# One PSUM bank instead of two pools for the latent head transposes of a two-layer hybrid decoder

## The chip, the core and the metric

The kernel runs on one core of one Trainium2 chip. The metric is the device time of one execution in microseconds (us). Five engines work beside each other, each through its own queue in program order: TensorE (PE, the matrix engine; its weight loads are listed as PEld), VectorE (DVE), ScalarE (ACT), GpSimd (POOL) and SyncE (SP), which issues most DMAs. PE writes its results to PSUM, which the kernel divides into eight tiles of 128 partitions by 512 floats, one bank each.

## What is computed

Two layers, each with a norm, one wide projection, three token mixers (a gated short convolution, multi-head latent attention, dilated window attention), gates, and an output projection with a residual. 512 tokens, width 1024. The part around the change is the latent attention, eight heads with 96 columns for queries and keys and 64 for values:

```
q = (rmsnorm(c_q, q_a_norm_g) @ w_uq).reshape(B, S, MLA_HEADS, MLA_QK)
kv = (rmsnorm(c_kv, kv_a_norm_g) @ w_ukv).reshape(B, S, MLA_HEADS, MLA_NOPE + MLA_V)
k_nope, v = jnp.split(kv, [MLA_NOPE], axis=-1)
k = jnp.concatenate([k_nope, jnp.broadcast_to(k_pe[:, :, None, :], ...)], axis=-1)
q = rmsnorm(q, mla_q_norm_g)
k = rmsnorm(k, mla_k_norm_g)
...rotary embedding on the last 32 columns of q and k...
o_b = causal_block_attention(q, k, v, MLA_QK ** -0.5)
```

## The kernel before

Matrix products are made from three matmuls (lines 124 to 126) on operands that are split into a rounded high part (`hi`, a cast on ACT) and a remainder (`lo`, a subtraction on DVE).

**Heads in pairs.** For each of the four head pairs `p`, `mla_p1` projects queries, keys and values and normalizes them with tokens on the partitions, and `mla_p2` turns queries and keys so that the 96 columns lie on the partitions. `mla_p2` makes four steps: the queries of head 0 (called q0 below), its keys (k0), the queries of head 1 (q1), its keys (k1). A step is four PE transposes into one PSUM tile (line 490), then a scaled cast on ACT that reads the tile (`hi`, line 494), then a scaled subtraction on DVE that reads it too (`lo`, line 495). The tile can be written again when line 495 is done. After each step `mla_p2` yields.

**What lies between the steps.** PE's order is written out by hand and is the same whatever the tiles are. A generator `filler` holds the wide projections (three matmuls of 512 columns for each advance). In the first `mla_p2` of a layer (`p` = 0, before the attention loop) two advances stand between steps. The other three run inside `mla_main`, which mixes scores (`mla_scores`), transposes of the probabilities (`mla_trans`, line 526), products with the values (`mla_pv`) and one step of `mla_p1` or `mla_p2` at a time, with one or two advances of `filler` between any two. The order on ACT, DVE and POOL is set by a scheduler at build time, by priorities.

**PSUM.** One pool with five tags gives the eight banks: `pj` two (projections), `sc` two (scores), `tr` two, `pv` one, `p1` one. `tr` holds the transposed probabilities, the query steps of `mla_p2`, the dilated queries (`dil_t`, line 680, its first half) and some small work. `p1` holds the products of `mla_p1`, the key steps of `mla_p2` and the dilated keys. In the trace and in the order below `p1` is written `p`, since numbers at a name's end are left out.

In the stretch that matters, a query step and the next key step use different banks, so PE can transpose the keys while ACT and DVE still read the queries. The probabilities and the query steps share the two `tr` banks in turn.

```
def psum(tag):
    return pp.tile([P, 512], F32, tag=tag, name=nm(tag), bufs=1 if tag in ("pv", "p1") else 2)
```

Of the kernel before, what the change touches and what calls it, by code (L numbers as in the profile page):

```python
# [49 lines left out]
def hybrid_kernel(ctx: ExitStack, tc: tile.TileContext, a: dict):  # L50
# [13 lines left out]
    def nm(s):  # L64
        uid[0] += 1
        return f"{s}_{uid[0]}"

    def psum(tag):
        return pp.tile([P, 512], F32, tag=tag, name=nm(tag), bufs=1 if tag in ("pv", "p1") else 2)
# [4 lines left out]
    def t2(shape, dt=F32):  # L74
        return sp.tile(shape, dt, tag="c2", name=nm("c2"), bufs=C2)
# [90 lines left out]
    def tok_nat(c):  # L166
        return slice(c * P, (c + 1) * P)
# [47 lines left out]
    ps = psum("tr")  # L215
# [6 lines left out]
    for l in range(DEPTH):  # L222
# [257 lines left out]
        def mla_p2(p):  # L480
            m = mla[p]
            for h in range(2):
                qk = []
                m["qk"].append(qk)
                for i in range(2):
                    ps = psum("p1" if i else "tr")
                    for c in range(NCH):
                        o = (2 * (p % 2) + h) * 96
                        src = m["kv"][c // 2][:, c % 2, h * P:h * P + 96] if i else m["q"][:, c, o:o + 96]
                        nc.tensor.transpose(ps[:96, tok_nat(c)], src, ident)  # L490
                    g = prm[:96, O_MK:O_MK + 1] if i else prm2[:96, 27:28]
                    hi, lo = t2([P, S], F32R), t2([P, S], F32R)
                    qk += [hi, lo]
                    nc.scalar.activation(hi[:96], ps[:96], AF.Copy, scale=g)
                    nc.vector.scalar_tensor_tensor(out=lo[:96], in0=ps[:96], scalar=g, in1=hi[:96],
                                                   op0=ALU.mult, op1=ALU.subtract)
                    yield
# [59 lines left out]
        def mla_main():  # L557

            prep = iter(())

            def more():
                if next(prep, "end") is None:
                    yield False

            for n in range(32 + LAG + PV_LAG + 1):
                for p in range(1, 4):
                    if n == P1_AT[p - 1]:
                        drain(prep)
                        mla_prep_w(p)
                        prep = mla_p1(p)  # L570
                    if n == P2_AT[p - 1]:
                        drain(prep)
                        prep = mla_p2(p)
                if n < 32:
                    mla_scores(n)
                    yield n >= N_TAIL
                yield from more()
                if 0 <= n - LAG < 32:
                    mla_trans(n - LAG)
                    yield n >= N_TAIL  # L580
                yield from more()
                i = n - LAG - PV_LAG
                if 0 <= i < 32 and i % 2 == 1:
                    mla_pv(i // 2)
                    yield n >= N_TAIL
# [435 lines left out]
        for _ in mla_p2(0):  # L1021
            advance(fill, 2)
# [19 lines left out]
        for dt in range(KD):  # L1042
# [4 lines left out]
            ps = psum("pj")  # L1047
# [103 lines left out]
```

## Time and profile before

| | |
|---|---|
| median of 3 runs | 1430.21 us (1429.95 to 1430.77) |
| the profiled execution | 1431.0 us, its span 1429.2 us |
| PE busy | 1419.2 us, 99% of the span |
| DVE, ACT, POOL busy | 874.0, 696.9, 121.4 us (61%, 49%, 8%) |
| DMA | 136.53 MB, 34.0% of the engines' time on the main queue |
| TensorE clock | granted share 0.998 over the run |
| chain of work that ended last | PE 92%, DVE 3% |

In a timeline row stand the start in us from the span's start, the duration in us, the engine, the line, the operation, and the tiles (out<-in) with shapes and count. A last bracket, where there is one, gives the time for which the engine sat idle just before and what it waited for. Rows of equal instructions that follow each other are merged into one; PE rows overlap since matmuls are pipelined.

### The profile page before, as it was taken

Reading aid. Unit: us, or ns where it says so; the run is one execution under the profiler, and the core shown is the slowest. Engines: PE = TensorE matmul, PEld = TensorE weight load, DVE = VectorE, ACT = ScalarE, POOL = GpSimd, SP = SyncE. Lnnn points to the kernel's source line nnn. Section 1 sums busy time; section 2 is a strip of 40 time slices with the busy share of each in tenths; the row PEclk is TensorE's granted clock in tenths of the full one; section 3 lists DMA queues with packets and bytes.
Section 4 is the critical chain, followed back from the end, with each engine's and each line's share of the span. In section 5 each row is a group of like instructions: output and inputs, shape, how many; then the busy total and the mean of one; then the engine's idle time right before and its main releaser. Section 6 shows DMA issues by size and latency. Waiting matters only on the chain.

```text
span 1429.2 us, 20412 instructions
## 1 busy us (share of the span) xinstructions
PE 1419.2 (99%) x7258; PEld 1174.1 (82%) x7258; DVE 874.0 (61%) x2298; ACT 696.9 (49%) x1587; POOL 121.4 (8%) x149
## 2 busy tenths in 40 slices
PE   9999999999999999999999999999999999999998
PEld 8888888888787878788898888888878878787887
DVE  7786877466363766455576858865654647564441
ACT  7445556573554554233354455666536455442330
POOL 0021211101010100000000202220010001000000
PEclk9999999999999999999999999999999999999999
DMA  8233232243242333232542322322432433233322
GB/s 256 81 104 88 64 88 76 74 119 89 74 120 57 94 104 90 74 120 86 183 120 77 107 63 75 89 60 75 119 101 77 119 89 90 75 91 87 104 74 89
DMA packets 237958, 136.53 MB, mean 96 GB/s; under 512 B 19872, under 2 KB 229664, under 8 KB 237856
## 3 DMA queue, kind: packets, MB, share of 16 engines
q1 hardware_dynamic: 237424, 134.80, 34.0%
q8 instruction: 57, 0.93, 0.3%
q10 hardware_dynamic: 432, 0.42, 0.1%
q14 instruction: 45, 0.37, 0.1%
HBM read 128.58 MB, written 6.62 MB: 95 GB/s over the span
## 4 chain that ended last, share of the span: by engine, by line
PE 92%; DVE 3%; issue 0%; ACT 0%; DMA 0%; DVEq 0%; POOL 0%; ACTq 0%
PE pj L124 26%; PE pj L126 25%; PE pj L125 25%; PE pv L847 2%; PE pv L543 1%; PE sc L735 1%; PE tr L526 1%; DVE wlo L119 1%; PE tr L816 1%; PE sc L125 1%; PE sc L126 1%; PE sc L124 1%; PE tr L680 1%; PE p L680 1%; PE p L126 1%; PE p L124 1%
## 5 line engine op out<-in xcount | busy, mean ns | idle before, releaser
L119 DVE TENSOR_TENSOR wlo<-wraw,whi 128x1024 fp32r<-128x1024 f32 (+1 forms) x223 | 270.6, 1218 | 185.5 <-ACT whi L118 182.5
L118 ACT CAST whi<-wraw 128x1024 fp32r<-128x1024 f32 (+1 forms) x223 | 229.9, 1033 | 252.4 <-PE pj L125 145.0
L124 PE MATMUL pj<-hhi,whi 128*128 128x512 f32 x760 | 307.4, 404 | 0.0
L126 PE MATMUL pj<-hhi,wlo 128*128 128x512 f32 x760 | 297.6, 392 | 0.0
L125 PE MATMUL pj<-hlo,whi 128*128 128x512 f32 x760 | 297.2, 391 | 0.2 <-DVE hlo L314 0.2
L124 PE MATMUL pj<-whi,hhi 128*128 128x512 f32 x576 | 237.0, 412 | 0.0
L126 PE MATMUL pj<-whi,hlo 128*128 128x512 f32 x576 | 225.8, 392 | 0.0
L125 PE MATMUL pj<-wlo,hhi 128*128 128x512 f32 x576 | 225.0, 391 | 0.0
L126 PEld LDWEIGHTS pj<-hhi,wlo 128*128 128x128 f32 x760 | 142.6, 188 | 30.9
L124 PEld LDWEIGHTS pj<-hhi,whi 128*128 128x128 f32 x760 | 143.0, 188 | 28.0 <-issue 1.7
L125 PEld LDWEIGHTS pj<-hlo,whi 128*128 128x128 f32 x760 | 143.2, 188 | 24.5 <-DVE hlo L314 0.9
L124 PE MATMUL pj<-c,whi 128*128 128x512 f32 x328 | 130.5, 398 | 0.0
L126 PEld LDWEIGHTS pj<-whi,hlo 128*128 128x128 f32 x576 | 108.1, 188 | 24.3
L126 PE MATMUL pj<-c,wlo 128*128 128x512 f32 x328 | 128.0, 390 | 0.0
L125 PE MATMUL pj<-c,whi 128*128 128x512 f32 x328 | 127.8, 389 | 0.0
L124 PEld LDWEIGHTS pj<-whi,hhi 128*128 128x128 f32 x576 | 108.4, 188 | 20.2 <-issue 1.0
L125 PEld LDWEIGHTS pj<-wlo,hhi 128*128 128x128 f32 x576 | 108.7, 189 | 17.2
L746 ACT ACTIVATE c<-c,e 128x128 f32<-128x128 f32 (+1 forms) x192 | 80.0, 418 | 30.8 <-DVE e L743 30.4
L668 POOL TENSOR_TENSOR c<-c,s16c 128x512 f32<-128x512 f32 x48 | 55.5, 1176 | 464.5 <-DVE s16c L107 287.1
L743 DVE CUSTOM_DVE_ANT_0 c<-sc,bias 128x128 f32<-128x128 f32 (+1 forms) x192 | 52.3, 319 | 39.2 <-PE sc L729 33.3
L124 PEld LDWEIGHTS pj<-c,whi 128*128 128x128 f32 x328 | 61.6, 188 | 14.0 <-issue 1.4
L126 PEld LDWEIGHTS pj<-c,wlo 128*128 128x128 f32 x328 | 61.6, 188 | 13.1
(207 smaller groups left out, 1941.3 us busy)
## 6 DMA issues: line engine op xcount, KB each, us to landing
wraw<-w_in SPq DMA_DIRECT2D x96, 512.0 KB, 3.8
wraw<-w_in SPq DMA_DIRECT2D x96, 192.0 KB, 2.9
wraw<-w_in SPq DMA_DIRECT2D x144, 128.0 KB, 2.8
wraw<-w_o SPq DMA_DIRECT2D x16, 512.0 KB, 4.0
bias<-bias SPq DMA_DIRECT2D x8, 512.0 KB, 4.2
wraw<-w_out_a SPq DMA_DIRECT2D x8, 512.0 KB, 4.7
wraw<-w_out_b SPq DMA_DIRECT2D x8, 512.0 KB, 3.4
wraw<-w_out_c SPq DMA_DIRECT2D x8, 512.0 KB, 3.3
```

The lines of the kernel that those rows point to most:

```text
L118: nc.scalar.copy(hi[:, c], raw[:, c])
L119: nc.vector.tensor_sub(lo[:, c], raw[:, c], hi[:, c])
L124: nc.tensor.matmul(out, lhs[0], rhs[0], start=start, stop=False)
L125: nc.tensor.matmul(out, lhs[0], rhs[1], start=False, stop=False)
L126: nc.tensor.matmul(out, lhs[1], rhs[0], start=False, stop=stop)
L526: nc.tensor.transpose(pst[:, tok_nat(j)], pr[:, tok_nat(j)], ident)
L543: nc.tensor.matmul(po[:, qo:256], vhl[j][:, hh, :], pt[t][j // 2][:, j % 2, qo:256], start=(j == 0 and t == 0), stop=(j == nj - 1 and t == 1))
L668: eng.tensor_tensor(out=nv[:, i:i + 8], in0=nv[:, i:i + 8], in1=r2[:, i:i + 8].unsqueeze(2).to_broadcast([P, 8, 64]), op=ALU.mult)
L680: nc.tensor.transpose(dst, nat[:, c, i * P:(i + 1) * P], ident)
L743: nc.vector.tensor_tensor_reduce(dst, src, b, op0=ALU.add, op1=ALU.min, scale=1.0, scalar=HIGHEST, accum_out=mc)
L746: nc.scalar.activation(dst, dst, AF.Exp, bias=mc, scale=-1.0, accum_out=sc_)
L847: nc.tensor.matmul(out, vs[g][:, c, hs[h]], rhs, start=(g == 0 and c == 0), stop=(g == 2 and c == 3), skip_group_check=True)
```

## The change

The query steps of `mla_p2` take their tile from `p1`, as the key steps do. Nothing else in the source is changed.

```
@@ mla_p2
                 for i in range(2):
-                    ps = psum("p1" if i else "tr")
+                    ps = psum("p1")
                     for c in range(NCH):
                         o = (2 * (p % 2) + h) * 96
```

On PE, ACT, POOL and SP the instructions stand in the same order as before; what differs on PE is what some of them wait for. Below, names in brackets are the engines whose progress an instruction waits for, `c` are tiles in SBUF, and a row with - is from before, with + from the changed kernel.

PE, layer 0, first `mla_p2`, the step q1:

```order
 L125 MATMUL pj_899<-hlo,whi_895 128x512
 L126 MATMUL pj_899<-hhi,wlo_896 128x512
-L490 MATMUL tr_921<-ident,c_124_647 96x128 [waits PE_49]
-L490 MATMUL tr_921<-ident,c_124_647 96x128 x3
+L490 MATMUL p_173_921<-ident,c_124_647 96x128 [waits DVE_49]
+L490 MATMUL p_173_921<-ident,c_124_647 96x128 x3
 L124 MATMUL pj_899<-hhi,whi_895 128x512
 L125 MATMUL pj_899<-hlo,whi_895 128x512
```

The step stands where it stood; it waits for DVE, which has to be done with the tile of k0, where it waited for nothing outside PE.

PE, layer 0, second `mla_p2`, in the attention loop: a transposition of probabilities and then the step k0.

```order
 L125 MATMUL pj_1173<-hlo,whi_1169 128x512
 L126 MATMUL pj_1173<-hhi,wlo_1170 128x512
-L526 MATMUL tr_1208<-ident,c_218_1118 128x128 [waits DVE_49,PE_49,Pool_49]
+L526 MATMUL tr_1208<-ident,c_218_1118 128x128 [waits Pool_49]
 L526 MATMUL tr_1208<-ident,c_218_1118 128x128 x3
 L124 MATMUL pj_1173<-hhi,whi_1169 128x512
 L125 MATMUL pj_1173<-hlo,whi_1169 128x512
 L126 MATMUL pj_1173<-hhi,wlo_1170 128x512
-L490 MATMUL p_241_1220<-ident,c_192_984 96x128 [waits Activation_49,Pool_49]
+L490 MATMUL p_241_1220<-ident,c_192_984 96x128 [waits DVE_49,Pool_49]
 L490 MATMUL p_241_1220<-ident,c_192_984 96x128
 L490 MATMUL p_241_1220<-ident,c_193_985 96x128 [waits Pool_49]
```

The probabilities no longer wait for DVE, and the step k0 waits for DVE in place of ACT.

DVE has its instructions in another order at two places, in the fourth `mla_p2` of each layer. In layer 0 it is the subtraction of k0, among the small steps of a reciprocal square root (`rs_t`, `s16c`):

```order
 L105 SCALAR_TENSOR_TENSOR rs_t_2265<-s16c_2256,s16b_2255 128x16
 L106 TENSOR_TENSOR rs_t_2265<-rs_t_2265,s16c_2256 128x16
+L107 SCALAR_TENSOR_TENSOR s16c_2256<-rs_t_2265,s16c_2256 128x16
+L105 SCALAR_TENSOR_TENSOR rs_t_2265<-s16c_2256,s16b_2255 128x16
 L495 SCALAR_TENSOR_TENSOR c_505_2357<-p_503_2351,prm_104,c_504_2356 96x512
-L107 SCALAR_TENSOR_TENSOR s16c_2256<-rs_t_2265,s16c_2256 128x16
+L106 TENSOR_TENSOR rs_t_2265<-rs_t_2265,s16c_2256 128x16
 L511 ISA c_507_2367,mst_2368<-sc_2363,mask 128x512
 L511 ISA mst_2368 128x1
-L105 SCALAR_TENSOR_TENSOR rs_t_2265<-s16c_2256,s16b_2255 128x16
-L106 TENSOR_TENSOR rs_t_2265<-rs_t_2265,s16c_2256 128x16
```

The subtraction stands two small instructions later. In layer 1 the subtraction of q1 stands three small ones later.

## Rows read from the trace of the kernel before

**Rows 1.** The page: the span, and PE's busy time (share, instructions).

```profile
span 1429.2 us, 20412 instructions
PE 1419.2 (99%) x7258; PEld 1174.1 (82%) x7258; DVE 874.0 (61%) x2298; ACT 696.9 (49%) x1587; POOL 121.4 (8%) x149
```

**Rows 2.** Timeline of layer 0, first `mla_p2`: PE steps, then DVE subtractions.

```profile
88.48 0.60 PE L490 MATMUL p<-ident,c 128*96 128x128 f32 x4
...
90.30 0.60 PE L490 MATMUL tr<-ident,c 128*96 128x128 f32 x4
...
92.12 0.60 PE L490 MATMUL p<-ident,c 128*96 128x128 f32 x4
...
88.83 0.74 DVE L495 SCALAR_TENSOR_TENSOR c<-tr,prm,c 96x512 fp32r<-96x512 f32 x1
89.83 0.75 DVE L495 SCALAR_TENSOR_TENSOR c<-p,prm,c 96x512 fp32r<-96x512 f32 x1 [0.26 <-ACT c L494]
```

**Rows 3.** Timeline of layer 0: PE's waits for a `tr` bank, and DVE before the longer.

```profile
114.47 0.63 PE L526 MATMUL tr<-ident,c 128*128 128x128 f32 x4 [0.57 <-DVE c L179]
...
169.91 0.30 PE L526 MATMUL tr<-ident,c 128*128 128x128 f32 x1 [1.50 <-DVE c L179]
...
169.35 0.42 DVE L179 TENSOR_TENSOR c<-tr,c 128x256 fp32r<-128x256 f32 x1
```

**Rows 4.** Timeline of layer 0, attention loop: step k0 of pairs 1 to 3, q0's subtraction.

```profile
115.63 0.60 PE L490 MATMUL p<-ident,c 128*96 128x128 f32 x4
...
115.18 0.74 DVE L495 SCALAR_TENSOR_TENSOR c<-tr,prm,c 96x512 fp32r<-96x512 f32 x1
...
171.44 0.60 PE L490 MATMUL p<-ident,c 128*96 128x128 f32 x4
...
172.13 0.74 DVE L495 SCALAR_TENSOR_TENSOR c<-tr,prm,c 96x512 fp32r<-96x512 f32 x1
...
212.61 0.60 PE L490 MATMUL p<-ident,c 128*96 128x128 f32 x4
...
212.72 0.74 DVE L495 SCALAR_TENSOR_TENSOR c<-tr,prm,c 96x512 fp32r<-96x512 f32 x1
```

**Rows 5.** Timeline of layer 1: a step on PE, the subtraction of the step ahead.

```profile
797.42 0.60 PE L490 MATMUL tr<-ident,c 128*96 128x128 f32 x4
...
797.78 0.74 DVE L495 SCALAR_TENSOR_TENSOR c<-p,prm,c 96x512 fp32r<-96x512 f32 x1
...
822.12 0.60 PE L490 MATMUL p<-ident,c 128*96 128x128 f32 x4
...
822.56 0.74 DVE L495 SCALAR_TENSOR_TENSOR c<-tr,prm,c 96x512 fp32r<-96x512 f32 x1
...
876.58 0.60 PE L490 MATMUL p<-ident,c 128*96 128x128 f32 x4
...
877.06 0.74 DVE L495 SCALAR_TENSOR_TENSOR c<-tr,prm,c 96x512 fp32r<-96x512 f32 x1
...
920.99 0.60 PE L490 MATMUL tr<-ident,c 128*96 128x128 f32 x4
...
921.22 0.75 DVE L495 SCALAR_TENSOR_TENSOR c<-p,prm,c 96x512 fp32r<-96x512 f32 x1
```

**Rows 6.** Timeline of layer 1, third pair: steps q1 and k1, the subtractions ahead.

```profile
879.81 0.60 PE L490 MATMUL tr<-ident,c 128*96 128x128 f32 x4
...
882.54 0.60 PE L490 MATMUL p<-ident,c 128*96 128x128 f32 x4
...
880.20 0.74 DVE L495 SCALAR_TENSOR_TENSOR c<-p,prm,c 96x512 fp32r<-96x512 f32 x1
...
883.00 0.75 DVE L495 SCALAR_TENSOR_TENSOR c<-tr,prm,c 96x512 fp32r<-96x512 f32 x1 [0.41 <-ACT c L494]
```

**Rows 7.** Stretches: length, busy us of PE, PEld, DVE, ACT, POOL, granted clock, DMA.

```profile
8.00:12.00 4.00, 4.00 (x15) 3.83 (x14) 3.95 (x6) 4.00 (x8) 0.00 (x0) 0.57 1.05 388
167.00:172.00 5.00, 3.50 (x21) 2.65 (x20) 5.00 (x17) 3.39 (x8) 0.80 (x1) 1.00 0.18 51
```

More of the change, by code (lines that the diff above doesn't have):

```diff
@@ L485, in mla_p2 @@
                 for i in range(2):
-                    ps = psum("p1" if i else "tr")
+                    ps = psum("p1")
                     for c in range(NCH):
```

## The prediction

> **What bounds the kernel now.** The page is read first: PE is busy for 1419.2 of 1429.2 us [rows 1], so PE's queue, which runs in order, sets the time, and DVE and ACT matter only where PE waits for them. The list of waits comes next, filtered to PE: what it lists on the transposed probabilities' account is what this change could give back. Two such places count: 0.57 us at 114.47 and 1.50 us at 169.91, both ended by DVE reading a `tr` bank (line 179) [rows 3]. That is 2.1 us, 0.15% of the span. The last view is the timeline of each of the eight passes of `mla_p2` (four pairs, two layers) on PE and DVE: what the reader is to see is when a step of four transposes starts on PE, and when DVE's subtraction of the step before it ends. Today these two don't touch each other, since neighbouring steps lie in different banks. After the change they do.
>
> **What the change removes.** The query steps leave the two `tr` banks. The probabilities then find the other bank of the two, which DVE had left long before, so the waits at 114.47 and 169.91 go [rows 3]. Up to 2.1 us in all, if nothing takes their place.
>
> **What it adds.** All four steps of a pass now follow each other in one bank, so each step but the first waits until line 495 of the step ahead is done. No transpose, cast, subtraction or DMA is added. Behind the waiting transposes stands everything else that PE does, the wide projections too, for PE doesn't pass a waiting instruction; a wait there is lost time in full, unless a later wait of PE shrinks by it. I cost each gap as: end of the subtraction, plus 0.14 us for the hand-over, less the start that the next step has now. The 0.14 us is from the place where PE waits for DVE today: line 179 ends at 169.35 + 0.42 = 169.77, PE starts at 169.91 [rows 3].
>
> First the pass ahead of the loop in layer 0 [rows 2]. q0's subtraction ends at 88.83 + 0.74 = 89.57, so k0 can start at 89.71 instead of 88.48: 1.23 us. Then the plain path shows its length: from k0's start to the end of its subtraction there are 89.83 + 0.75 - 88.48 = 2.10 us, with the hand-over 2.24, in which ACT and DVE hardly wait for anything but this step. The steps are spaced by 90.30 - 88.48 = 1.82 and 92.12 - 90.30 = 1.82 us. So q1 and k1 each come 0.42 us too early, and the pass costs 1.23 + 2 x 0.42 = 2.07 us.
>
> In the attention loop the steps are further apart, and the plain path of 2.24 us would fit. But there DVE has other work in its queue ahead of line 495, so the subtraction comes late. For k0 of pairs 1, 2 and 3 [rows 4]: 115.18 + 0.74 + 0.14 - 115.63 = 0.43 us; 172.13 + 0.74 + 0.14 - 171.44 = 1.57 us; 212.72 + 0.74 + 0.14 - 212.61 = 0.99 us. These are absolute times, so the removed waits of 0.57 and 1.50 us are already in them: PE reaches k0 earlier by that much, and then waits there for DVE until the same moment. That is how the gain of the change is used up.
>
> Layer 1 [rows 5]. In the first pass q1 is late by 797.78 + 0.74 + 0.14 - 797.42 = 1.24 us, and k1 by another 0.42 by the plain path: 1.66 us. (A smaller delay of k0 there lies inside that, because DVE's queue and not PE holds k0's subtraction.) In the loop: 822.56 + 0.74 + 0.14 - 822.12 = 1.32 us, 877.06 + 0.74 + 0.14 - 876.58 = 1.36 us, and for the fourth pair, where q1 is the latest, 921.22 + 0.75 + 0.14 - 920.99 = 1.12 us.
>
> **The sum.** Layer 0: 2.07 + 0.43 + 1.57 + 0.99 = 5.06 us. Layer 1: 1.66 + 1.32 + 1.36 + 1.12 = 5.46 us. Together 10.5 us. In each pass I take the largest lateness once and let the later steps of the pass go free where their subtraction is held by DVE's queue and not by PE. That is the choice that matters; its other end is below. The two changed places on DVE's queue, where a subtraction stands two or three small instructions later, I cost at nothing: the next step on PE comes after them by more than the plain path, and if that cover were gone they would cost what two or three such instructions take there, under 0.5 us each. Later uses of the `p1` bank (the next pair's `mla_p1`, the dilated keys) start a few us after k1's subtraction and add nothing.
>
> Against the profiled execution, 1431.0 us with a span of 1429.2, the sum gives a span of 1439.7 and a time of 1441.5; against the median, 1430.2 + 10.5 = 1440.7 us. I use the median.
>
> Bounds of the unknown part, how far ACT and DVE follow PE when PE is late. Lower end: they don't follow, and use PE's waits to work off their queue, so that in the loop the plain path of 2.24 us always fits and only the two passes ahead of the loop pay, 3 x 0.42 us each: 2.5 us, less the 2.1 us of removed waits, +0.4 us. Upper end: they follow fully, and latenesses inside a pass add up. The third pair of layer 1 shows the most of it: q1 is late by 880.20 + 0.74 + 0.14 - 879.81 = 1.27 us and k1 by 883.00 + 0.75 + 0.14 - 882.54 = 1.35 us [rows 6] on top of the 1.36 of k0. With these, 2.6 us, and one each of 0.2 to 0.5 us in five other passes, 1.7 us together, it is 14.8 us. The sum of 10.5 is nearer to the rows, since the queues ahead of line 495 hold work (weight subtractions, convolution taps) that is itself paced by PE's projections, which argues against the lower end, and since a late step finds DVE's queue shorter, which argues against the upper.
>
> One rule speaks against this change. The Trainium skill, "Perfetto Trace Analysis", section "Optimizing Tensor Performance", says that independent groups of matmuls should rotate through different PSUM banks so that the evacuation of one overlaps the matmuls of the next. Taken alone it would have every step pay; the trace agrees for the passes ahead of the loop (path 2.24 us, spacing 1.82), while in the loop the spacing alone would pardon it and it is DVE's queue that decides.
>
> **The rivals.**
>
> *Latenesses add up* (upper end): all of a pass shifts with PE, 14.8 us, 1445.0 us. For it: DVE's queue is full through these stretches (5.00 of 5.00 us from 167 to 172 [rows 7]). Against it: in the passes ahead of the loop DVE sits idle between subtractions.
>
> *No change, not slower*: the queues on DVE and ACT drain while PE waits. A pass in the loop is then free when line 495 starts about 1.4 us after its step, as it does for k0 at 88.48 and 89.83 [rows 2]; from there on only the passes ahead of the loop cost, and the freed waits pay for them: +0.4 us, 1430.6 us. Against it: at 172.13 the subtraction of q0 is held by a queue that PE feeds, and PE is not ahead of it but behind. A faster kernel needs more still: that passes ahead of the loop also lose less than 2.1 us together.
>
> *The clock falls.* PE's granted clock was 0.57 from 8 to 12 us, that is, most of these 4 us at 1.2 GHz, just after PE had waited for its first operands; it stayed at 1.00 from 167 to 172 us around a wait of 1.50 us [rows 7]. The new waits are of that size, but in some passes several come close together. A stretch like that at the start loses 4 x (1 - 0.57) = 1.7 us; two of them on top of the sum give 10.5 + 3.4 = 13.9 us, 1444.1 us. The Trainium skill, "TensorE: Matmul & The Clock Gate", section "What's actually happening", has the throttled state as the default that activity releases; the rows at 8 to 12 us agree, and those at 167 to 172 us show a wait that did not bring it on.
>
> *The change doesn't do what it says* is excluded: the order shows the query steps on `p`, with DVE's wait.
>
> **How the numbers follow.** The forecast, +7 to +13 us around 10.5, has 0.66. Adding up has 0.12, the clock 0.08. A part of the loop draining, +3 to +7 us, has 0.06. No change has 0.06 and faster 0.02. About 0.2% (2.9 us) is what a measurement of this kernel can tell from no change, so slower has 0.66 + 0.12 + 0.08 + 0.06 = 0.92. The range goes from +6.3 to +16 us, 1436.5 to 1446.2: the forecast, nearly all of adding up, most of the clock's case.
>
> **What would show it.** In the changed kernel's list of waits of PE: a new entry, line 490 on `p` waiting for DVE line 495, some 11 to 15 times, 10 to 13 us in all, none above 2 us; the entry of line 526 waiting for line 179 gone or nearly so. PE's busy time should stay near 1419 us, the clock at 1.00 in the eight passes, and the time between the passes unchanged. In the passes ahead of the loop the steps should stand 2.24 us apart. I am wrong on the mechanism if the time grows while line 490 doesn't wait, and on the size if the waits in the loop are far from 0.4 to 1.6 us per pass.

## Result, and the profile after

The changed kernel takes 1443.9 us (median of 4 runs, 1440.7 to 1444.58) against 1430.37 us before (4 runs): 1.0089 times the time, 95% interval 1.0077 to 1.0101. The forecast was 1440.7 us in 1436.5 to 1446.2.

The page of the changed kernel shows the span 13.6 us longer, and PE's busy time up by 5.2 us though it does the same instructions, compared with [rows 1]:

```profile
span 1442.8 us, 20402 instructions
...
PE 1424.4 (99%) x7258; PEld 1175.3 (81%) x7258; DVE 875.5 (61%) x2298; ACT 697.5 (48%) x1587; POOL 121.2 (8%) x149
```

The first lines of its list of PE's waits (who waited <- for whom: us in total, times, longest):

```profile
PE p L490 <- DVE c L495: 7.9, 12, 1.8
PE p L490 <- POOL c L515: 3.1, 1, 3.1
PE sc L124 <- ACT whi L178: 1.3, 1, 1.3
```

Line 490 now waits in thirteen places, and line 526 in none. The second entry is DVE too, as is shown further down.

The first pass of layer 0, timeline of PE and then DVE, answers to [rows 2]:

```profile
89.51 0.61 PE L490 MATMUL p<-ident,c 128*96 128x128 f32 x4 [1.08 <-DVE c L495]
...
91.68 0.64 PE L490 MATMUL p<-ident,c 128*96 128x128 f32 x4 [0.17 <-DVE c L495]
...
93.88 0.64 PE L490 MATMUL p<-ident,c 128*96 128x128 f32 x4 [0.15 <-DVE c L495]
...
88.62 0.74 DVE L495 SCALAR_TENSOR_TENSOR c<-p,prm,c 96x512 fp32r<-96x512 f32 x1
...
90.88 0.75 DVE L495 SCALAR_TENSOR_TENSOR c<-p,prm,c 96x512 fp32r<-96x512 f32 x1 [1.51 <-ACT c L494]
```

The steps stand 2.17 and 2.20 us apart, where they stood 1.82 us apart. DVE, which the steps wait for, sat idle 1.51 us before the subtraction of k0, because the cast on ACT has to wait for the transposes: this is the plain path. From the end of a subtraction to the next step's start there were 0.15 us for k0 (89.36 to 89.51), but only 0.05 us for q1 (91.63 to 91.68).

Head pair 2 of layer 0, PE, DVE and POOL, answers to [rows 3, 4]:

```profile
170.51 0.27 PE L526 MATMUL tr<-ident,c 128*128 128x128 f32 x1
...
175.25 1.06 PE L490 MATMUL p<-ident,c 128*96 128x128 f32 x4 [3.09 <-POOL c L515]
...
173.17 1.22 DVE L119 TENSOR_TENSOR wlo<-wraw,whi 128x1024 fp32r<-128x1024 f32 x1
174.31 0.15 DVE L514 RECIPROCAL mst<-mst 128x1 f32<-128x1 f32 x1
174.38 0.73 DVE L495 SCALAR_TENSOR_TENSOR c<-p,prm,c 96x512 fp32r<-96x512 f32 x1
...
174.63 0.58 POOL L515 TENSOR_SCALAR c<-c,mst 128x384 f32<-128x384 f32 x1 [2.68 <-DVE mst L514]
```

The probabilities (line 526) start without a wait, and k0 waits 3.1 us. The profile names POOL's line 515, which ended 0.04 us before PE went on, at 175.21; but k0 does not use what that instruction writes, and in the kernel before k0 started at 171.44 [rows 4], ahead of that instruction, which started at 172.38 there. DVE's subtraction ended at 174.38 + 0.73 = 175.11, and PE went on 0.14 us later, the hand-over of [rows 3]. The k0 group took 1.06 us where it takes 0.6 elsewhere: the clock. Stretches around it (length, busy us of PE, PEld, DVE, ACT, POOL, granted clock, DMA) answer to [rows 7]:

```profile
168.00:174.00 6.00, 4.16 (x21) 3.06 (x20) 6.00 (x21) 3.95 (x10) 0.80 (x1) 1.00 0.35 86
174.00:181.00 7.00, 5.75 (x16) 4.68 (x17) 3.52 (x9) 1.64 (x4) 0.66 (x2) 0.52 0.32 77
```

From about 174 to 181 us the granted clock was at half, 1.2 GHz, for some 7 x 0.48 / 0.5 = 6.7 us of the second stretch. It fell while PE still waited: from 174.2 to 175.2 us, in which PE ran nothing, it was already 0.55 on average.

**Where the time went.** PE has the same 7258 instructions in the same order in both traces. For each I took its start in the changed kernel less its start before; the difference grows only at a few instructions. Its growth over each pass (where a wait of line 526 went away, the time gained there is counted in):

| pass | growth, us | of it, waits gone | predicted |
|---|---|---|---|
| layer 0, pair 0 | 2.00 | | 2.07 |
| layer 0, pair 1 | 0.45 | -0.76 | 0.43 |
| layer 0, pair 2 | 1.56 | -1.69 | 1.57 |
| layer 0, pair 3 | 0.97 | | 0.99 |
| layer 1, pair 0 | 1.56 | | 1.66 |
| layer 1, pair 1 | 1.84 | | 1.32 |
| layer 1, pair 2 | 1.56 | -0.36 | 1.36 |
| layer 1, pair 3 | 1.12 | | 1.12 |
| the eight passes | 11.1 | -2.8 | 10.5 |
| 175 to 181 us, no wait, longer matmuls | 2.70 | | - |

11.06 + 2.70 = 13.76 us; the changed kernel was 0.21 us ahead at 80 us, which leaves 13.55 of the 13.56 us at the last instruction. Between the passes and after the last one the two traces keep their distance to 0.05 us. (The expectations below put the eight passes at 10.8 us, 0.2 us lower than this table.) By the same comparison, 2.9 of the 5.2 us of additional busy time of PE lie around the fall of the clock; most of the rest lies at the other waits, about 0.2 us at each.

### The profile page after: what moved, and what is told of

Read it like the earlier page. It is cut to its first block, busy times and chain, and to the rows that moved or that the text cites. A ratio compares the mean times of both kernels' runs of the same rounds, so it can differ in the third digit from the quotient of the medians.

```text
span 1442.8 us, 20402 instructions
## 1 busy us (share of the span) xinstructions
PE 1424.4 (99%) x7258; PEld 1175.3 (81%) x7258; DVE 875.5 (61%) x2298; ACT 697.5 (48%) x1587; POOL 121.2 (8%) x149
## 4 chain that ended last, share of the span: by engine, by line
PE 90%; DVE 5%; ACT 1%; issue 1%; DMA 0%; POOL 0%; DVEq 0%; POOLq 0%
PE pj L124 25%; PE pj L126 24%; PE pj L125 24%; PE pv L847 2%; DVE wlo L119 2%; PE pv L543 1%; PE sc L735 1%; PE tr L526 1%; PE p L490 1%; PE tr L816 1%; PE sc L125 1%; PE sc L126 1%; PE sc L124 1%; PE tr L680 1%; PE p L680 1%; PE p L126 1%
```

## Experiments

The theory: one bank for all steps makes each step wait for the subtraction of the one before, which is late by the plain path ahead of the loop and by DVE's queue in it; and the 3.1 us wait of pair 2 in layer 0 brings the clock down. The rivals: the passes depend on each other, or part is given back; the queries' place in `p1` costs in itself; the fall of the clock has nothing to do with that one wait. Each kernel ran 5 or 11 times, beside the kernel before: 21 runs with a median of 1430.95 us (all but one pass, only the passes ahead of the loop, only those in it, the exchange) and 21 with 1430.86 us (the other four).

### All but one pass

```
-                    ps = psum("p1")
+                    ps = psum("tr" if not i and l == 0 and p == 2 else "p1")
```

> As the changed kernel, but the queries of head pair 2 in layer 0 keep their `tr` bank. Theory (one bank for all four steps of a pass makes each step wait for the subtraction of the step before it; the net cost of a pass can be read off as the growth of the distance between the two traces, +1.57 us for this pass; and the long wait there also brought the granted clock to half for 6.8 us, which cost another 2.7 us): the time is 1430.4 + (10.8 - 1.6) = about 1439.6 us, no granted clock of one half after the first 15 us, and the step k0 at about 176 us does not wait. Rival (the fall of the clock comes from the sum of all the small waits, or is chance, and not from this wait): the clock falls in about the same share of the runs, here or at another pass, and the time stays at 1442 to 1443 us.

1439.8 us (1439.33 to 1440.45), 1.0061 times before (1.0048 to 1.0073), +8.9 us. In its profiled run the clock is at full from 10 us to the tail. PE's longest waits, and the stretch in which the clock fell in the changed kernel:

```profile
PE p L490 <- DVE c L495: 7.8, 13, 1.6
PE tr L526 <- DVE c L179: 1.5, 1, 1.5
...
172.00:179.00 7.00, 7.00 (x37) 5.75 (x37) 5.71 (x15) 3.58 (x10) 1.28 (x2) 1.00 0.34 77
```

The wait of 3.1 us is gone, the wait of 1.5 us on `tr` is back, and the other passes cost what they cost in the changed kernel. So 13.5 - 8.9 = 4.6 us of the changed kernel's loss hang on this one pass, of which 1.56 are its lateness and 2.7, where the clock falls, the clock; the 0.3 us left are within the spread of the runs.

### Only the passes ahead of the loop, only those in it

```
-                    ps = psum("p1" if i else "tr")
+                    ps = psum("p1" if i or p == 0 else "tr")
```

> Only the first pass of each layer (head pair 0, ahead of the attention loop) has its queries in the keys' bank. Theory: three waits in each layer, net +1.93 us in layer 0 and +1.56 us in layer 1, as in the changed kernel: 1430.4 + 3.5 = 1433.9 us, clock at full. Rival (a wait of PE ahead of the loop is given back later, since DVE and ACT then have less queued when the loop begins): 1430 to 1432 us.

1434.49 us (11 runs), 1.0023 times (1.0013 to 1.0032), +3.5 us. PE's list of waits shows line 490 for 2.4 us in six places, and the three waits on `tr`, 2.2 us, as before. Nothing is given back later.

```
-                    ps = psum("p1" if i else "tr")
+                    ps = psum("p1" if i or p > 0 else "tr")
```

> Only the passes inside the attention loop (head pairs 1 to 3) have their queries in the keys' bank. Theory: the loop's passes cost what they cost in the changed kernel, net 0.49 + 1.57 + 0.90 in layer 0 and 1.79 + 1.57 + 1.03 in layer 1, 7.35 us: 1437.8 us where the clock stays at full, and 2.7 us more, 1440.5 us, where it falls at pair 2 of layer 0. Together with the run on the first passes alone the parts should add up to the whole, 10.8 us without the clock. Rival (the passes depend on each other: without the delay of the first pass DVE's queue lies otherwise and the waits in the loop are smaller): under 1436 us.

1438.6 us (1438.15 to 1441.21), 1.0056 times (1.0043 to 1.0068), +7.7 us. The two parts give 3.5 + 7.7 = 11.2 us, the whole without the clock was 11.1: the passes are nearly independent. In the profiled run k0 of pair 2 waited 3.1 us, and the clock stayed at full:

```profile
165.00:172.00 7.00, 5.43 (x28) 4.19 (x26) 7.00 (x23) 3.71 (x8) 2.00 (x3) 1.00 0.30 75
172.00:180.00 8.00, 6.50 (x36) 5.45 (x37) 5.54 (x13) 3.85 (x10) 1.28 (x2) 1.00 0.28 68
```

So the wait may bring the clock down in some executions and not in others. That needed an experiment of its own.

### Only the pass with the long wait

```
-                    ps = psum("p1" if i else "tr")
+                    ps = psum("p1" if i or (l == 0 and p == 2) else "tr")
```

> Only the pass of head pair 2 in layer 0 has its queries in the keys' bank. In the changed kernel its k0 waits once for 3.2 us, where the kernel before waited twice for 1.5 us in other places. Theory: net +1.57 us, 1432.5 us, in the runs in which the granted clock stays at full, and +2.7 us more, about 1435 us, in those in which the long wait brings it to half; both kinds should turn up, told apart by the clock of the stretch. Rival (the fall of the clock in the profiled run of the changed kernel has to do with the earlier, smaller waits as well): no run above 1434 us.

1433.41 us (11 runs), 1.0022 times (1.0013 to 1.0031). The runs fall into two groups by their mean granted clock: seven with 0.999 take 1432.53 to 1434.0 us, four with 0.996 take 1435.3 to 1435.57. The profiled run is of the second kind. Two lines of its list of PE's waits, and the clock:

```profile
PE p L490 <- POOL c L515: 3.1, 1, 3.1
...
PE tr L526 <- DVE c L179: 0.6, 1, 0.6
...
165.00:172.00 7.00, 4.98 (x25) 3.79 (x24) 7.00 (x22) 4.09 (x10) 1.58 (x3) 1.00 0.29 75
172.00:179.00 7.00, 5.91 (x17) 4.72 (x18) 3.35 (x9) 1.50 (x3) 0.82 (x2) 0.51 0.32 77
```

One wait of 3.1 us is enough, with no other in the pass; ahead of it in the loop stands only the wait of 0.6 us at 114 us, which the kernel before has too. By the mean clock and the time, 4 of 11 runs had the fall. The mean alone can mislead, because a stretch like that at 8 to 12 us [rows 7] lowers it as well, and only some executions have that stretch: the changed kernel's profile has 1.00 there. But a mean of 0.996 stands only in kernels with the wait of 3.1 us, in these four runs and in one of the loop-only kernel (1441.21 us); none of the 42 runs of the kernel before has it, and none of the 48 runs of the six other kernels.

The changed kernel fits in part. Of its four runs the one at 1440.7 us has a clock of 1.0 and the forecast's time without a fall. But a second run as slow as the profiled one, 1444.57 us, has a mean of 0.999, which leaves room for at most 0.0015 x 1442.8 / 0.5 = 4.3 us at half clock, and so not for the whole fall. In the profiled run the 2.7 us are the clock's; how much of the median is stays open.

### Queries and keys change places

```
-                    ps = psum("p1" if i else "tr")
+                    ps = psum("tr" if i else "p1")
```

> Queries in the single bank `p1`, keys in the two banks of `tr`: the two kinds change places against the kernel before, so neighbouring steps lie in different banks again, and the queries still are where the change put them. Theory (what costs is that neighbouring steps share one bank, not where the queries are): line 490 does not wait for DVE line 495 at all; and as the probabilities now share `tr` with the keys instead of the queries, the waits of line 526 at 114.47, 169.91 and 875.05 us go too, which gave 0.67 + 1.65 + 0.32 = 2.6 us in the changed kernel: 1427.8 us, faster than before. It could be up to 1430.5 us if the keys bring new waits of line 526. Rival (the queries in `p1` cost in themselves, by running into the products of the next pair's projection or the dilated keys): 1436 us or more.

1427.96 us (11 runs, 1427.31 to 1429.36), 0.9978 times before (0.9969 to 0.9987): faster than both kernels, by 3.0 us than before. All of PE's waits, whole list:

```profile
PE sc L124 <- ACT whi L178: 1.4, 1, 1.4
PE tr L217 <- POOL c L214: 1.0, 1, 1.0
PE sc L735 <- DVE e L743: 0.7, 2, 0.4
PE pj L125 <- DVE hlo L314: 0.2, 1, 0.2
```

Neither line 490 nor line 526 waits. Pair 2 of layer 0:

```profile
167.34 0.60 PE L490 MATMUL p<-ident,c 128*96 128x128 f32 x4
...
168.48 0.27 PE L526 MATMUL tr<-ident,c 128*128 128x128 f32 x1
...
170.16 0.61 PE L490 MATMUL tr<-ident,c 128*96 128x128 f32 x4
```

The queries are in `p1` here too, so their place costs nothing; that the keys follow them there is what costs. In the kernel before, a query step took a `tr` bank between two tiles of probabilities, and so sent the second to the bank that DVE was late with. Here it is the keys that come to that bank, later, when DVE is all but done with it: its line 179 ends at 170.02 us and k0 starts at 170.16, by the starts of PE's instructions 0.17 us late, too little for the list.

### The bank left after one read

```
+                    raw = t2([P, S])
-                    nc.scalar.activation(hi[:96], ps[:96], AF.Copy, scale=g)
-                    nc.vector.scalar_tensor_tensor(out=lo[:96], in0=ps[:96], scalar=g, in1=hi[:96],
-                                                   op0=ALU.mult, op1=ALU.subtract)
+                    nc.scalar.activation(raw[:96], ps[:96], AF.Copy, scale=g)
+                    nc.scalar.copy(hi[:96], raw[:96])
+                    nc.vector.tensor_sub(lo[:96], raw[:96], hi[:96])
```

> The changed kernel, all steps in one bank, but the bank is left after one read: ACT copies the scaled tile to SBUF, and the cast to `hi` (ACT) and the subtraction to `lo` (DVE) work on the copy. 32 more ACT instructions of about 0.7 us, beside PE. Theory (the wait lasts until line 495 has read the bank, and in the loop that is late because of DVE's queue, not because of the transposes or ACT): from a step's start to the end of ACT's first read there are 0.6 + 0.7 us, with the hand-over 1.45, under the spacing of 1.82 us, and in the loop ACT reads 2 to 3 us ahead of DVE where the lateness is largest. Line 490 then waits for ACT for under 1 us in all, the waits of line 526 stay gone: 1428 to 1429.5 us, the clock at full. Rival (the steps' bank costs in another way, such as running into other users of it): 1436 us or more.

1430.41 us (11 runs), 0.9997 times before (0.9988 to 1.0006), 13.5 us under the changed kernel. (Lines below 494 stand one lower in this kernel.) From the list of PE's waits:

```profile
PE p L490 <- ACT c L495: 0.9, 2, 0.5
PE sc L736 <- DVE e L744: 0.7, 2, 0.4
```

All steps are still in one bank, and the wait of line 490 for DVE is gone: it was DVE's late read that held the bank. The expected 1428 to 1429.5 us was not reached, because ACT's queue can hold the one read that is left. For k1 of pair 2 in layer 0, ACT and PE:

```profile
175.76 0.73 ACT L514 ACTIVATE c<-c,mst 128x512 f32<-128x512 f32 x1 [1.36 <-DVE mst L512]
...
176.48 0.67 ACT L495 ACTIVATE c<-p,prm 96x512 f32<-96x512 f32 x1
...
177.20 0.64 PE L490 MATMUL p<-ident,c 128*96 128x128 f32 x4 [0.37 <-ACT c L495]
```

ACT, which runs in order, waited 1.36 us for DVE's part of a softmax, and q1's read stood behind that; k1 starts when the read ends, at 177.15. By the starts of PE's instructions, five steps lose 2.0 us and one product of `mla_p1` 0.3 us against the kernel before, and line 526 gains 2.8: 0.5 us faster in sum, as the medians have it (1430.41 against 1430.86), which the interval can't tell from none.

### Steps further apart

```
         for _ in mla_p2(0):
-            advance(fill, 2)
+            advance(fill, 3)
```

> The changed kernel with three advances of the projections instead of two after each step of the first pass of a layer, so that its steps stand 1.82 + 0.69 = 2.51 us apart where the plain path of a step takes 2.2 us. The loop is shifted by four advances against the projections. Theory: the waits of the plain path, 0.35 + 0.37 us in layer 0 and 0.37 us and part of the others in layer 1, vanish; the first step's wait for a late subtraction shrinks by 0.69. The first passes fall from 3.5 to about 1 us, and the time by 2 to 2.5 us against the changed kernel, unless the shifted loop waits otherwise: 1438.5 us with the clock at full, 1441 with its fall. Rival (the wait is a fixed cost of sharing a bank, whatever the distance): no change, 1441 to 1444 us.

1440.12 us (1439.02 to 1442.53), 1.0067 times (1.0054 to 1.0079). In layer 0's first pass one wait is left of three (k0, 0.41 us, after 1.08), in layer 1 none of three. So the waits there depend on the distance, as the theory has it. The long wait of pair 2 shrank to 1.12 us, and the clock stayed at full there. The 1438.5 us expected at full clock were missed by 1.6 us; the loop, shifted by four advances against the projections, shows other waits, of which three from the list:

```profile
PE pv L543 <- DVE c L553: 1.1, 1, 1.1
...
PE pj L124 <- DVE c L968: 0.8, 1, 0.8
...
PE pj L124 <- ACT c L956: 0.5, 1, 0.5
```

### Both in the double bank

```
-                    ps = psum("p1" if i else "tr")
+                    ps = psum("tr")
```

> Queries and keys both take a `tr` bank, `p1` is left to the projections of pairs and the dilated keys. Neighbouring steps lie in two banks in turn, with the probabilities between them. Theory (what counts is how many uses of a bank lie between a step and its bank's next use): in the first passes, no wait, as before. In the loop a step and the transposition of probabilities that follows it take both banks, so that k0 comes back to the bank that q0 had, or probabilities meet a bank that waits for DVE: waits on line 526 and line 490 together of 3 to 9 us, all in the loop, 1431 to 1437 us. Rival (any two banks in turn are as good as the kernel before): 1430 to 1431 us.

1437.68 us (1436.32 to 1438.76), 1.0047 times (1.0034 to 1.0059), +6.8 us, 0.7 us above the range that was expected. The passes ahead of the loop cost nothing, those in the loop 6.7 us, close to their 7.5 in the changed kernel: between q0 and k0 stands one tile of probabilities, so that in a pool of two k0 comes back to q0's bank. Pair 2 of layer 0:

```profile
170.34 0.30 PE L526 MATMUL tr<-ident,c 128*128 128x128 f32 x1 [1.51 <-DVE c L179]
...
173.43 0.61 PE L490 MATMUL tr<-ident,c 128*96 128x128 f32 x4 [1.40 <-POOL c L515]
...
172.00:179.00 7.00, 5.60 (x31) 4.67 (x31) 4.61 (x11) 3.20 (x10) 1.28 (x2) 1.00 0.32 77
```

Here PE waits 2.9 us in two pieces for the same lateness, with 1.7 us of work between, and the clock stays at full. Of the other four runs, three have a mean clock of 1.0, and the last has the profiled run's clock and time. Five runs are few: if the fall came here in 4 of 11 too, all five would be without it about one time in ten.

## Why the prediction was right, and where it was off

**What bounds the kernel, and what the change removes**: right. PE sets the time, the waits of line 526 went, and they were 2.8 us instead of 2.1 (a third, smaller one had been left out, and PE's gaps are shorter in the list than what the starts of its instructions lose, 1.69 against 1.50 us for the longest).

**The first passes**: right. The plain path was forecast at 2.24 us and stands at 2.17 and 2.20, since the hand-over of 0.14 us that the sum took everywhere was 0.05 us at q1 and k1; 2.07 and 1.66 us against 2.00 and 1.56. The run with only these passes gave 3.5 us.

**The passes in the loop**: right in kind and nearly in size. The rule "largest lateness once, the rest free" held in five of six passes to 0.2 us; pair 1 of layer 1 had a second wait, at k1, that cost 0.41 us and that the rule left out. The two subtractions that moved on DVE's queue, costed at nothing, show no cost: their passes measured 0.97 and 1.12 us against 0.99 and 1.12. The lower bound, that queues drain while PE waits, is refuted by the loop-only run (+7.7 us), and the upper one, that latenesses add up (14.8 us), by the 11.1 us.

**The removed waits are used up**: right. In pair 2 of layer 0 PE came earlier to k0 by 1.69 us and waited there until DVE's subtraction had ended, so that the pass costs 1.56 us net, as forecast.

**The term that was missing**: the clock, 2.7 us. It stood among the rivals with 0.08, with the sentence that the new waits are of the size of 1.50 us, around which the clock had stayed at full. That step failed. The paragraph on the loop had both numbers: if the wait of 1.50 us moves to k0, which is late by 1.57 us, there is one wait of 3.1 us, of a size that the trace before did not have. The runs show what this does: with one such wait alone the clock falls to half in 4 of 11 runs, and with the same lateness in two pieces in none of 5, as far as their clocks show. The price that the rival named, 1.7 us per stretch, was too small, since the stretch lasted about 7 us and not 4. That the rival's total of 1444.1 us lies next to the measured 1443.9 is luck: it counted two stretches, and there was one. The measured +13.5 us lies just above the forecast's own +7 to +13, and inside the range because that had room for this rival and for latenesses that add up.

**The signs**: thirteen waits and 11.0 us fit the 11 to 15 and 10 to 13 that were named; "none above 2 us" and the clock at 1.00 in all passes did not hold, both through that one wait, nor did PE's busy time "near 1419 us", for a little over half by the fall of the clock.

## What to carry to other kernels

What a shared bank costs can be read off a trace beforehand, place by place: the end of its last reader, plus the hand-over, less the start that the next writer has now; here PE, busy for 99% of the span and running its queue in order, paid it in full. Ask not how many banks a pool has but what stands between two uses of one bank: the same three banks gave 1428, 1430, 1438 and 1444 us, depending on which tiles follow each other. And when a change moves a wait to where another begins, add them up and ask what one long wait does to TensorE's clock.

## What the runs showed of the hardware

A single wait of 3.1 us in a busy stretch of TensorE went with some 7 us of granted clock at half, 1.2 GHz, in some executions (0.51 and 0.52 over 7 us in two profiles), beginning before the wait was over, and with none in another (1.00 in the loop-only run). It cost 2.7 us in the changed kernel's profile and makes the kernel with one such wait have two times, 1432.5 to 1434.0 and 1435.3 to 1435.6 us. Two waits of 1.5 and 1.4 us with 1.7 us of work between them left the clock at full in the profiled run; five runs can't show that it always does. What decides between the executions stays open.
